# Gate and up by seven half-size products of sums of blocks, and down in a second pass

## The chip, the cores and the metric

The kernel runs on one core of one Trainium2 chip. The metric is the device time of an execution in microseconds (us). Engines are named as the profile names them: PE is TensorE's matmuls and PEld its weight loads, DVE is VectorE, ACT is ScalarE, POOL is GpSimd, SP is SyncE, which here only issues transfers.

## What is computed

One decoder layer in float32 for 512 tokens of width 2048: two kinds of attention side by side, their joint projection added to x, and then the feed-forward part, which is what the change touches:

```
x = x + mixed @ w_out[l]

h = rms_norm(x, ffn_norm_w[l])
x = x + (jax.nn.silu(h @ w_gate[l]) * (h @ w_up[l])) @ w_down[l]
return rms_norm(x, final_norm_w)
```

w_gate and w_up are 2048 x 5632, w_down is 5632 x 2048.

## The kernel before

Every product of float32 numbers is made as three matmuls in fp32r (mm3, line 143): each operand is split into a rounded part and a rest, and rounded x rounded, rounded x rest and rest x rounded are added in PSUM. For a weight the split is load_w (line 117): SP starts a transfer of 128 x 1024 floats (512 KB) into one of two buffers `raw`, ACT casts it to `whi` (line 137), DVE subtracts to get `wlo` (line 138); there are three pairs of whi and wlo, so a split can run ahead of PE by two loads.

x after attention (x2) lies in SBUF with tokens on partitions, 4 tiles of 128. out_part (line 714) adds the last pieces of the joint projection, 128 x 512 at a time; its last call is for four chunks of 512 columns. x2_split (line 857) transposes a chunk of x2 on PE, scales it by ffn_norm_w and splits it into `fh`, `fl`: features of the model on partitions, 512 tokens along the row. The division by the norm is left to later: `rbc` holds it for each token along a row, `rstd` for each token on a partition.

The feed-forward part goes by 11 groups of 512 hidden features. gate_up (line 884) takes a group in two pairs of 256 features, gate first and then up; I call gate or up of 256 features a unit, and there are 44. A unit loads four pieces of weights and makes 2 x 16 x 3 = 96 matmuls of 512 columns into two banks. Evicting a gate is a product with rbc on DVE and a Silu on ACT, evicting an up is a product with the gate and a split into `ah`, `al`. down (line 914) follows one group behind: for each chunk of 512 output columns two loads of w_down, 48 matmuls, and four additions to x2 on DVE. The last group of down is fused with the final norm.

What each engine does is a queue in the order that the program's scheduler made of the code; an instruction that waits holds up what stands behind it. ACT has casts, evictions and a few transfers in one queue, DVE splits and evictions, SP the transfers of weights. A tile's buffer is taken again when its last reader is over, in the order of the code.

Of the kernel before, what the change touches and what calls it, by code (L numbers as in the profile page):

```python
# [9 lines left out]
F32 = mybir.dt.float32  # L10
# [79 lines left out]
def layer_kernel(ctx: ExitStack, tc: tile.TileContext, x, positions, w_in, a_log, dt_bias, w_uq, w_ukv,  # L90
# [51 lines left out]

    def mm3(ps, lh, ll, rh, rl, start, stop):
        nc.tensor.matmul(ps, lhsT=lh, rhs=rh, start=start, stop=False)  # L144
        nc.tensor.matmul(ps, lhsT=lh, rhs=rl, start=False, stop=False)  # L145
        nc.tensor.matmul(ps, lhsT=ll, rhs=rh, start=False, stop=stop)  # L146

# [36 lines left out]
    def pool(stack, name, bufs=1, side=None):  # L184
        return stack.enter_context(tc.tile_pool(name=name, bufs=bufs, side=side, reuse_waits="tile"))
# [118 lines left out]

    ba = const.tile([P, NT, 16], F32, name="ba")

# [19 lines left out]

    sc = const.tile([P, 10, NT, NH], F32, name="sc")
    ea, tt_, ab, e_, z_, pl, beta, g_, gc, dec = (sc[:, i] for i in range(10))
    egc = const.tile([P, NT, NH], F32, name="egc")
    egl = const.tile([P, NT, NH], F32, name="egl")  # L330

# [363 lines left out]
    banks(op=1, score=3, acc=2, bank=2)  # L695
    x2 = pool(right, "x2", side="right").tile([P, NT, D], F32, name="x2")
# [4 lines left out]
    mgp = {"b": pool(mla_right, "mgb", side="right")}  # L701
    for c in range(4):
# [144 lines left out]
    mla_left.close()  # L847
    mix_stack.close()


    banks(acc=4, bank=4)
    fpool = pool(left, "ffn")
    fh = fpool.tile([P, KD, S], F32R, name="fh")
    fl = fpool.tile([P, KD, S], F32R, name="fl")
    jo = fpool.tile([P, S], F32, name="jo")
# [12 lines left out]
    mla_right.close()  # L868


    ap_ = pool(left, "act", bufs=2)
    fin = ap_.tile([P, D], F32, name="fin", bufs=1)
    nc.scalar.dma_start(fin, final_norm_w.rearrange("(o d) -> o d", o=1).broadcast_to([P, D]))

    def x2_rstd():
        nc.vector.tensor_reduce(out=st4[:, 0:4], in_=ssx, op=ALU.add, axis=AX.X)
        nc.vector.tensor_scalar(out=st4[:, 0:4], in0=st4[:, 0:4], scalar1=1.0 / D, scalar2=EPS,
                                op0=ALU.mult, op1=ALU.add)
        rsq(rstd, st4[:, 0:4])
        rows_of(ap_, rstd, rbc, "dg")  # L880

    NG = NFF // 4

    def gate_up(g):
        ah = ap_.tile([P, 4, S], F32R, name="ah", tag="ah")
        al = ap_.tile([P, 4, S], F32R, name="al", tag="al")
        for pr in range(2):
            c0 = g * S + pr * 256
            gs = []
            for w_v in (wg_v, wu_v):  # L890
                a2 = [acc() for _ in range(2)]
                for kk in range(4):
                    if g == 0 and pr == 0 and w_v is wg_v and kk == 3:
                        x2_split(3)
                        x2_rstd()
                    wh, wl = load_w(w_v[:, 4 * kk:4 * kk + 4, c0:c0 + 256], 4, 256)
                    for f in range(2):
                        fs = slice(f * P, (f + 1) * P)
                        for j in range(4):
                            k = 4 * kk + j  # L900
                            mm3(a2[f], wh[:, j, fs], wl[:, j, fs], fh[:, k, :], fl[:, k, :], k == 0, k == KD - 1)
                for f in range(2):
                    if w_v is wg_v:
                        s = ap_.tile([P, S], F32, name="sg", tag="sg", bufs=4)
                        nc.vector.tensor_tensor(out=s, in0=a2[f], in1=rbc, op=ALU.mult)
                        nc.scalar.activation(s, s, AF.Silu)
                        gs.append(s)
                    else:
                        s = gs[f]
                        nc.vector.tensor_tensor(out=s, in0=a2[f], in1=s, op=ALU.mult)  # L910
                        split(ah[:, 2 * pr + f, :], al[:, 2 * pr + f, :], s)
        return ah, al

# [12 lines left out]

    prev = None
# [74 lines left out]
```

## Time and profile before

| | before |
|---|---|
| runs | 2427.9, 2429.2, 2432.1 us, median 2429.2 |
| profiled execution | 2431.8 us, span of the records 2430.0 us |
| PE, PEld | 2377.5 us (98%), 1954.5 us (80%) |
| DVE, ACT, POOL | 1137.5 us (47%), 706.8 us (29%), 84.6 us (3%) |
| read from HBM | 219.5 MB, 92 GB/s over the span |

Busy time of an engine is the time in which one of its instructions ran; for PE the ends of matmuls are modelled, and they overlap, so the distance from one start to the next is the price of one in a stream, not its duration. In the feed-forward part, from 978 us on, gate and up take 44 units and down 11 groups; the last group with the final norm begins at 2375 us.

### The profile page before, as it was taken

The page shows a single profiled execution, that of the slowest core. Times are in us where ns is not written, and L with a number is a line of the kernel's source. Part 1 is how long each engine was busy: PE and PEld are TensorE (multiplying, and loading weights), DVE is VectorE, ACT ScalarE, POOL GpSimd, SP SyncE. Part 2 cuts the span into 40 slices and gives each one's busy share as a digit, 9 for nine tenths or more (in the row PEclk, how much of TensorE's full clock was granted, in tenths as well). Part 3 has the DMA queues.
Part 4 walks back from the last instruction along what each step waited for, and adds up shares of the span by engine and source line. Part 5 has one row for each costly group of instructions (what it writes and reads, how often), then busy time and mean ns, then how long its engine had stood idle before and what let it go on. Part 6 is the DMA issues. An engine that isn't in the chain of part 4 may idle for free.

```text
span 2430.0 us, 27609 instructions
## 1 busy us (share of the span) xinstructions
PE 2377.5 (98%) x11142; PEld 1954.5 (80%) x11142; DVE 1137.5 (47%) x1850; ACT 706.8 (29%) x1155; POOL 84.6 (3%) x89
## 2 busy tenths in 40 slices
PE   8999999999999999999999999999999999999998
PEld 6777878787787778888888888888888888888886
DVE  6556565655556555433434343433333343434345
ACT  5333333332333334322222212222222222222223
POOL 0010101110000000000000000000000000000000
PEclk9999999999999999999999999999999999999999
DMA  5322322222422222333333333232333333333333
GB/s 168 89 62 70 88 70 80 78 80 78 143 61 67 73 65 87 104 96 100 99 95 96 96 95 101 90 104 87 104 93 103 98 96 95 95 97 95 104 96 112
DMA packets 199807, 225.74 MB, mean 93 GB/s; under 512 B 17280, under 2 KB 161920, under 8 KB 199552
## 3 DMA queue, kind: packets, MB, share of 16 engines
q1 hardware_dynamic: 194752, 214.02, 29.4%
q10 hardware_dynamic: 4928, 9.97, 1.3%
q8 instruction: 87, 1.43, 0.3%
q14 instruction: 40, 0.33, 0.0%
HBM read 219.50 MB, written 4.46 MB: 92 GB/s over the span
## 4 chain that ended last, share of the span: by engine, by line
PE 87%; DVE 6%; DMA 3%; ACT 2%; issue 1%; POOL 1%; ACTq 0%; SPq 0%; POOLq 0%; DVEq 0%
PE acc L145 20%; PE acc L146 20%; PE acc L144 20%; PE bank L145 6%; PE bank L146 6%; PE bank L144 6%; PE bank L149 4%; DVE wlo L138 1%; PE score L149 1%; DMA rep<-dr 1%; DMA raw<-in_w_down 1%; PE op L149 1%; DVE y L444 1%; DMA raw<-in_w_in 1%; ACT whi L137 0%
## 5 line engine op out<-in xcount | busy, mean ns | idle before, releaser
L138 DVE TENSOR_TENSOR wlo<-raw,whi 128x1024 fp32r<-128x1024 f32 x386 | 469.0, 1216 | 705.7 <-ACT whi L137 701.0
L137 ACT CAST whi<-raw 128x1024 fp32r<-128x1024 f32 x386 | 403.6, 1046 | 1195.2 <-PE acc L145 650.0
L145 PE MATMUL acc<-fl,whi 128*128 128x512 f32 x1408 | 548.3, 389 | 0.0
L146 PE MATMUL acc<-fh,wlo 128*128 128x512 f32 x1408 | 548.2, 389 | 0.0
L144 PE MATMUL acc<-fh,whi 128*128 128x512 f32 x1408 | 548.1, 389 | 0.0
L145 PEld LDWEIGHTS acc<-fl,whi 128*128 128x128 f32 x1408 | 264.4, 188 | 54.8
L146 PEld LDWEIGHTS acc<-fh,wlo 128*128 128x128 f32 x1408 | 264.4, 188 | 54.8
L144 PEld LDWEIGHTS acc<-fh,whi 128*128 128x128 f32 x1408 | 264.3, 188 | 54.5
L145 PE MATMUL acc<-hl,whi 128*128 128x512 f32 (+1 forms) x656 | 264.4, 403 | 0.0
L144 PE MATMUL acc<-hh,whi 128*128 128x512 f32 (+1 forms) x656 | 262.1, 400 | 1.8 <-ACT whi L137 1.8
L146 PE MATMUL acc<-hh,wlo 128*128 128x512 f32 (+1 forms) x656 | 263.6, 402 | 0.0
L146 PE MATMUL bank<-whi,al 128*128 128x512 f32 x640 | 249.2, 389 | 0.0
L145 PE MATMUL bank<-wlo,ah 128*128 128x512 f32 x640 | 249.2, 389 | 0.0
L144 PE MATMUL bank<-whi,ah 128*128 128x512 f32 x640 | 249.2, 389 | 0.0
L924 DVE SCALAR_TENSOR_TENSOR x<-bank,rstd,x 128x512 f32<-128x512 f32 x160 | 119.8, 750 | 151.6 <-PE bank L146 151.6
L144 PEld LDWEIGHTS acc<-hh,whi 128*128 128x128 f32 (+1 forms) x656 | 124.3, 190 | 25.7 <-ACT whi L137 2.2
L145 PEld LDWEIGHTS acc<-hl,whi 128*128 128x128 f32 (+1 forms) x656 | 124.3, 190 | 24.5
L146 PEld LDWEIGHTS acc<-hh,wlo 128*128 128x128 f32 (+1 forms) x656 | 123.9, 189 | 23.5
L144 PEld LDWEIGHTS bank<-whi,ah 128*128 128x128 f32 x640 | 120.2, 188 | 24.9
L145 PEld LDWEIGHTS bank<-wlo,ah 128*128 128x128 f32 x640 | 120.2, 188 | 24.9
L146 PEld LDWEIGHTS bank<-whi,al 128*128 128x128 f32 x640 | 120.2, 188 | 24.9
L144 PE MATMUL acc<-whi,mgh 128*128 128x512 f32 x256 | 102.3, 400 | 2.8 <-ACT mgh L283 2.3
(284 smaller groups left out, 2228.1 us busy)
## 6 DMA issues: line engine op xcount, KB each, us to landing
raw<-in_w_gate SPq DMA_DIRECT2D x88, 512.0 KB, 3.6
raw<-in_w_up SPq DMA_DIRECT2D x88, 512.0 KB, 3.6
raw<-in_w_down SPq DMA_DIRECT2D x88, 512.0 KB, 3.8
raw<-in_w_in SPq DMA_DIRECT2D x80, 512.0 KB, 3.8
raw<-in_w_out SPq DMA_DIRECT2D x32, 512.0 KB, 4.0
rep<-dr ACTq DMA_DIRECT2D x8, 512.0 KB
x<-in_x ACTq DMA_DIRECT2D x4, 1024.0 KB, 7.8
raw<-in_w_ukv SPq DMA_DIRECT2D x32, 128.0 KB, 2.5
```

The source lines that it names most:

```text
L137: nc.scalar.copy(hi[:, :k * n], raw[:, :k * n])
L138: nc.vector.tensor_tensor(out=lo[:, :k * n], in0=raw[:, :k * n], in1=hi[:, :k * n].bitcast(F32), op=ALU.subtract)
L144: nc.tensor.matmul(ps, lhsT=lh, rhs=rh, start=start, stop=False)
L145: nc.tensor.matmul(ps, lhsT=lh, rhs=rl, start=False, stop=False)
L146: nc.tensor.matmul(ps, lhsT=ll, rhs=rh, start=False, stop=stop)
L149: nc.tensor.matmul(ps, lhsT=l, rhs=r, start=start, stop=stop)
L444: nc.vector.scalar_tensor_tensor(out=y, in0=u[:, j:j + S], scalar=vec[:, 0, j * 24 + ct:j * 24 + ct + 1], in1=y, op0=ALU.mult, op1=ALU.add)
L924: nc.vector.scalar_tensor_tensor(out=x2[:, t4, cs], in0=a, scalar=rstd[:, t4:t4 + 1], in1=x2[:, t4, cs], op0=ALU.mult, op1=ALU.add)
```

## The change

The product of a unit, 256 features by 2048 by 512 tokens, is written as a product of 2 x 2 blocks: the weights' two halves of features by even and odd blocks of the contraction, the activations' even and odd blocks by two halves of the tokens. Such a product is made with seven products of blocks in place of eight: four sums of weight blocks (s1 to s4), four sums of activation blocks (made once for all units), and seven sums of results, of which some are made by going on adding in a bank (`further` marks this in mm3). Each of the seven is 8 x 3 = 24 matmuls of 256 columns.

The seven activation operands, split, take 114 KB of each partition (`ch`, `cl`). So x2 is stored in DRAM (x2d), the products of gate and up are too (actd, a tile for each group), and down runs when all units are over: each group's activations are loaded and split (act_group), x2 is loaded again, and then down and the tail are as before. A unit's weights come in four transfers into one of two large buffers (wraw, 2 MB).

Left out of the diff: four small tiles (ba, sc, egc, egl) that move from one pool to another, the pool of mgb, which now outlives ckv, and mm3's new argument.

```
+    banks(acc=2, x=2, y=1, z=1, bank=2)
+    ch = cb.tile([P, N7, KD // 2, H], F32R, name="ch")
+    cl = cb.tile([P, N7, KD // 2, H], F32R, name="cl")
...
-    def x2_split(c):
-        for k in range(4 * c, 4 * c + 4):
+    def operands(i):
+        tps = []
+        for k in (2 * i, 2 * i + 1):
             tp = bank()
             for t4 in range(NT):
                 nc.tensor.transpose(tp[:, t4 * P:(t4 + 1) * P], x2[:, t4, k * P:(k + 1) * P], ident)
-            split(fh[:, k, :], fl[:, k, :], tp, fw[:, k:k + 1])
+            tps.append(tp)
+        st = tr.tile([P, N7, H], F32, name="stg", tag="stg", bufs=1)
+        wa, wb = fw[:, 2 * i:2 * i + 1], fw[:, 2 * i + 1:2 * i + 2]
+        nc.scalar.mul(st[:, 0, :], tps[0][:, 0:H], wa)
+        nc.scalar.mul(st[:, 5, :], tps[0][:, H:S], wa)
+        nc.scalar.mul(st[:, 1:3, :].rearrange("p a n -> p (a n)"), tps[1], wb)
+        for o, x, y in ((3, 5, 0), (5, 2, 5), (4, 2, 3), (6, 1, 4)):
+            nc.vector.tensor_tensor(out=st[:, o, :], in0=st[:, x, :], in1=st[:, y, :], op=ALU.subtract)
+        split(ch[:, :, i, :], cl[:, :, i, :], st)
 
     for c in range(4):
         out_part(12, mg_b, c, jo)
+        nc.scalar.dma_start(x2d[c].rearrange("p (t n) -> p t n", t=NT), x2[:, :, c * S:(c + 1) * S])
         if c:
-            x2_split(c - 1)
+            operands(2 * c - 2)
+            operands(2 * c - 1)
+    operands(6)
+    operands(7)
...
+    def unit(w_v, c0, dst):
+        raw = wr.tile([P, KD, 2 * P], F32, name="wraw", tag="wraw")
+        for kk in range(4):
+            nc.sync.dma_start(raw[:, 4 * kk:4 * kk + 4, :], w_v[:, 4 * kk:4 * kk + 4, c0:c0 + 2 * P])
...
+        def product(ps_, w, m, start=False):
+            hi = wp.tile([P, 1024], F32R, name="whi", tag="whi").rearrange("p (i n) -> p i n", n=P)
+            lo = wp.tile([P, 1024], F32R, name="wlo", tag="wlo").rearrange("p (i n) -> p i n", n=P)
+            split(hi, lo, w)
+            for i in range(KD // 2):
+                mm3(ps_, hi[:, i, :], lo[:, i, :], ch[:, m, i, :], cl[:, m, i, :],
+                    start and i == 0, i == KD // 2 - 1, not start)
...
+        product(X, a11, 0, True)
+        p1 = kept(X, "p1")
+        s1 = sum_of(a21, a22, ALU.add)
+        s2 = sum_of(s1, a11, ALU.subtract, "sw")
+        product(Z, a12, 1, True)
+        added(0, 0, Z, p1)
+        product(X, s2, 4)
+        u2 = kept(X, "u2")
+        product(Y, s1, 3, True)
+        p5 = kept(Y, "p5")
+        product(X, sum_of(a11, a21, ALU.subtract), 5)
+        added(1, 1, X, p5)
+        product(Y, sum_of(a12, s2, ALU.subtract), 2)
+        added(0, 1, Y, u2)
+        product(X, a22, 6)
+        nc.scalar.copy(dst[:, 1, 0:H], X)
...
+    for u in range(NFF // 2):
+        g, o = divmod(u, 2)
+        s = gu.tile([P, 2, S], F32, name="sg", tag="sg", bufs=2)
+        unit(wg_v, u * 2 * P, s)
...
+        nc.scalar.activation(s, s, AF.Silu)
+        t = gu.tile([P, 2, S], F32, name="up", tag="up")
+        unit(wu_v, u * 2 * P, t)
+        nc.vector.tensor_tensor(out=s, in0=t, in1=s, op=ALU.mult)
+        nc.scalar.dma_start(actd[g].rearrange("p (k n) -> p k n", n=S)[:, 2 * o:2 * o + 2, :], s)
...
+    def act_group(g):
+        ah = ad.tile([P, 4, S], F32R, name="ah", tag="ah")
+        al = ad.tile([P, 4, S], F32R, name="al", tag="al")
+        v = actd[g].rearrange("p (k n) -> p k n", n=S)
+        for o in (0, 2):
+            dst = tuple(t_[:, o:o + 2, :].rearrange("p k n -> p (k n)") for t_ in (ah, al))
+            load_w(v[:, o:o + 2, :], 2, S, dst)
+        return ah, al
+    cur = act_group(0)
...
+    for c in range(4):
+        nc.scalar.dma_start(x2[:, :, c * S:(c + 1) * S], x2d[c].rearrange("p (t n) -> p t n", t=NT))
...
-    for g in range(NG):
-        cur = gate_up(g)
-        if prev is not None:
-            down(g - 1, *prev)
-        prev = cur
+    for g in range(NG - 1):
+        nxt = act_group(g + 1)
+        down(g, *cur)
+        cur = nxt
```

Here kept copies a bank to SBUF on ACT, added adds such a copy and a bank on DVE into the unit's result, and sum_of adds or subtracts two weight blocks on DVE; ad holds two buffers each of ah and al.

Three places show what stands in the queues. On SP, from the last gate and up on, before:

```order
L135 DMA raw<-in_w_up 128x4x256 x4
L135 DMA raw<-in_w_down 128x2x512 x8
L135 DMA raw<-in_w_gate 128x4x256 x4
L135 DMA raw<-in_w_up 128x4x256 x4
L135 DMA raw<-in_w_gate 128x4x256 x4
L135 DMA raw<-in_w_up 128x4x256 x4
L135 DMA raw<-in_w_down 128x2x512 x16
```

and on SP for the last groups of down in the change (actd is the tile of one group's activations in DRAM):

```order
L135 DMA raw<-in_w_down 128x2x512 x8
L135 DMA raw<-actd_7538 128x1024 x2
L135 DMA raw<-in_w_down 128x2x512 x8
L135 DMA raw<-actd_7539 128x1024 x2
L135 DMA raw<-in_w_down 128x2x512 x8
L135 DMA raw<-actd_7540 128x1024 x2
L135 DMA raw<-in_w_down 128x2x512 x16
```

Down's weights no longer alternate with those of gate and up, but with the next group's activations, through the same two buffers. On ACT in the change, from the last weights of down(0) to the first of down(1); in brackets are the engines and transfer queues (DMAHW) that each waits for:

```order
L137 CAST whi<-raw 128x1024 [waits DMAHW4_49,DVE_49,PE_49]
L137 CAST whi<-raw 128x1024 [waits DMAHW5_49,DVE_49,PE_49]
L137 CAST ah<-raw 128x1024 [waits DMAHW6_49,PE_49]
L137 CAST ah<-raw 128x1024 [waits DMAHW7_49]
L137 CAST whi<-raw 128x1024 [waits DMAHW0_49,DVE_49]
L137 CAST whi<-raw 128x1024 [waits DMAHW1_49,DVE_49]
L137 CAST whi<-raw 128x1024 [waits DMAHW2_49,DVE_49,PE_49]
```

The two casts of the next group's activations (ah) stand ahead of down(1)'s first weights, and the first of them waits for PE. On ACT where gate and up begin, before (fh is the split of x2's last chunk):

```order
L286 ACTIVATE fh<-bank,vec 128x512 x4
L137 CAST whi<-raw 128x1024 x4
L286 ACTIVATE fh<-bank,vec 128x512 x4
L906 ACT_TABLE_LOAD
L906 ACTIVATE sg<-sg 128x512
```

and in the change (stg is the staging tile of operands, vec the norm's weights):

```order
L882 ACTIVATE stg<-bank,vec 128x256
L883 ACTIVATE stg<-bank,vec 128x256
L884 ACTIVATE stg<-bank,vec 128x512
L284 CAST ch<-stg 128x7x256
L882 ACTIVATE stg<-bank,vec 128x256
L883 ACTIVATE stg<-bank,vec 128x256
L884 ACTIVATE stg<-bank,vec 128x512
L284 CAST ch<-stg 128x7x256
L284 CAST whi<-wraw 128x1024 x2
L284 CAST whi<-sw 128x1024
```

Where casts of gate weights stood ahead of the last split of x2, all operands now stand ahead of the first weights.

## Rows read from the trace of the kernel before

**Rows 1.** The page: busy time by engine, granted clock in 40 slices, chain by engine.
```profile
PE 2377.5 (98%) x11142; PEld 1954.5 (80%) x11142; DVE 1137.5 (47%) x1850; ACT 706.8 (29%) x1155; POOL 84.6 (3%) x89
...
PEclk9999999999999999999999999999999999999999
...
PE 87%; DVE 6%; DMA 3%; ACT 2%; issue 1%; POOL 1%; ACTq 0%; SPq 0%; POOLq 0%; DVEq 0%
```

**Rows 2.** Timeline of gate and up: start, duration (us), engine, line, operation, out<-in.
```profile
978.60 0.39 PE L144 MATMUL acc<-fh,whi 128*128 128x512 f32 x1
...
984.94 0.39 PE L145 MATMUL acc<-fl,whi 128*128 128x512 f32 x1
...
1043.57 0.69 DVE L905 TENSOR_TENSOR sg<-acc,rbc 128x512 f32<-128x512 f32 x1 [0.64 <-PE acc L146]
...
1065.33 0.69 DVE L910 TENSOR_TENSOR sg<-acc,sg 128x512 f32<-128x512 f32 x1 [0.63 <-PE acc L146]
```

**Rows 3.** Timeline of PE in v_pair, 21 rows between.
```profile
667.02 0.28 PE L145 MATMUL acc<-wlo,ckh 128*128 128x256 f32 x1
...
669.66 0.28 PE L146 MATMUL acc<-whi,ckl 128*128 128x256 f32 x1
```

**Rows 4.** Instructions by line and shape: count | busy us, mean ns of one.
```profile
L138 DVE TENSOR_TENSOR wlo<-raw,whi 128x1024 fp32r<-128x1024 f32 x380 | 464.6, 1223 | 691.9 <-ACT whi L137 687.3 <-PE bank L861 4.2
...
L571 DVE TENSOR_TENSOR R<-R,bank 128x256 f32<-128x256 f32 x16 | 6.7, 421 | 23.6 <-PE bank L149 23.6
...
L137 ACT CAST whi<-raw 128x1024 fp32r<-128x1024 f32 x380 | 399.7, 1052 | 1160.7 <-PE acc L145 641.4 <-PE bank L146 248.9 <-issue 196.6
...
L556 ACT COPY T<-bank 64x256 f32<-64x256 f32 x8 | 2.9, 365 | 24.2 <-PE bank L555 24.2
```

**Rows 5.** Timeline: x2's load, and the passage from out_part to gate.
```profile
632.54 2.20 ACTq L703 DMA_DIRECT2D x<-in_x  x4
...
977.26 0.68 DVE L723 TENSOR_TENSOR x<-acc,x 128x512 f32<-128x512 f32 x1
...
978.67 2.40 ACT L286 ACTIVATE fh<-bank,vec 128x512 fp32r<-128x512 f32 x4
...
1003.45 0.69 DVE L905 TENSOR_TENSOR sg<-acc,rbc 128x512 f32<-128x512 f32 x1 [1.80 <-PE acc L146]
```

**Rows 6.** Timeline of the tail; transfers of L135, landing after issue.
```profile
2379.35 1.23 DVE L138 TENSOR_TENSOR fl<-raw,fh 128x1024 fp32r<-128x1024 f32 x1 [2.13 <-ACT fh L137]
...
2380.60 0.37 SPq L135 DMA_DIRECT2D raw<-in_w_down  x1
...
2382.98 0.50 PE L144 MATMUL bank<-fh,ah 128*128 128x512 f32 x1 [0.92 <-ACT fh L137]
...
2384.43 1.05 ACT L137 CAST fh<-raw 128x1024 fp32r<-128x1024 f32 x1 [0.88 <-DMA raw<-in_w_down]
...
DMA to landing us min/median/max: 3.3/3.7/11.0
```

**Rows 7.** Window: length, busy us by engine, granted clock, DMA share, GB/s.
```profile
8.00:12.00 4.00, 2.85 (x14) 2.85 (x15) 1.30 (x3) 1.53 (x3) 0.00 (x0) 1.00 1.08 377
```

**Rows 8.** Timeline of PE at the start and the end, and a window.
```profile
14.59 0.79 PE L144 MATMUL acc<-hh,whi 128*128 128x512 f32 x1 [1.77 <-ACT whi L137]
...
16.04 0.63 PE L145 MATMUL acc<-hl,whi 128*128 128x512 f32 x1
16.46 0.63 PE L146 MATMUL acc<-hh,wlo 128*128 128x512 f32 x1
...
21.13 0.39 PE L144 MATMUL acc<-hh,whi 128*128 128x512 f32 x1
21.36 0.39 PE L145 MATMUL acc<-hl,whi 128*128 128x512 f32 x1
...
2420.48 0.39 PE L146 MATMUL bank<-fh,al 128*128 128x512 f32 x1
...
2424.00:2428.00 4.00, 0.00 (x0) 0.00 (x0) 0.48 (x2) 0.93 (x2) 0.00 (x0) 0.50 0.78 253
```

More of the change, by code (lines that the diff above doesn't have):

```diff
@@ L141, in load_w, with mm3 @@
                 lo[:, :k * n].rearrange("p (k n) -> p k n", k=k))
[L143 to L146, printed above, removed]
+    def mm3(ps, lh, ll, rh, rl, start, stop, further=False):
+        nc.tensor.matmul(ps, lhsT=lh, rhs=rh, start=start, stop=False, skip_group_check=further)
+        nc.tensor.matmul(ps, lhsT=lh, rhs=rl, start=False, stop=False, skip_group_check=further)
+        nc.tensor.matmul(ps, lhsT=ll, rhs=rh, start=False, stop=stop, skip_group_check=further)
     def mm(ps, l, r, start=True, stop=True):
@@ L302, in row @@
         return gd.tile([P, S], F32, name="s_" + name, tag=name, bufs=bufs)
-    ba = const.tile([P, NT, 16], F32, name="ba")
+    ba = gd.tile([P, NT, 16], F32, name="ba", tag="ba", bufs=1)
     def narrow():
@@ L695, in layer_kernel @@
     banks(op=1, score=3, acc=2, bank=2)
-    x2 = pool(right, "x2", side="right").tile([P, NT, D], F32, name="x2")
+    x2_stack = right.enter_context(ExitStack())
+    x2 = pool(x2_stack, "x2", side="right").tile([P, NT, D], F32, name="x2")
+    mix_right = right.enter_context(ExitStack())
+    mgp = {"b": pool(mix_right, "mgb", side="right")}
     mla_right = right.enter_context(ExitStack())
@@ L700, in layer_kernel @@
     ckl = ckp.tile([P, NT, S], F32R, name="ckl")
-    mgp = {"b": pool(mla_right, "mgb", side="right")}
     for c in range(4):
@@ L848, in layer_kernel @@
     mix_stack.close()
[L851 to L855, printed above, removed]
-    def x2_split(c):
-        for k in range(4 * c, 4 * c + 4):
+    mla_right.close()
+    banks(acc=2, x=2, y=1, z=1, bank=2)
+    H = S // 2
+    N7 = 7
+    dram2 = ctx.enter_context(tc.tile_pool(name="dram2", bufs=1, space=bass.MemoryType.DRAM))
+    x2d = [dram2.tile([P, NT * S], F32, name=f"x2d{c}", tag=f"x2d{c}") for c in range(4)]
+    NG = NFF // 4
+    actd = [dram2.tile([P, 4 * S], F32, name=f"actd{g}", tag=f"actd{g}") for g in range(NG)]
+    cb_stack = left.enter_context(ExitStack())
+    cb = pool(cb_stack, "cb")
+    ch = cb.tile([P, N7, KD // 2, H], F32R, name="ch")
+    cl = cb.tile([P, N7, KD // 2, H], F32R, name="cl")
+    tr_stack = left.enter_context(ExitStack())
+    tr = pool(tr_stack, "tr")
+    jo = tr.tile([P, S], F32, name="jo", tag="jo", bufs=1)
+    def operands(i):
+        tps = []
+        for k in (2 * i, 2 * i + 1):
             tp = bank()
@@ new lines, in layer_kernel @@
+    operands(6)
+    operands(7)
+    nc.vector.tensor_reduce(out=st4[:, 0:4], in_=ssx, op=ALU.add, axis=AX.X)
+    nc.vector.tensor_scalar(out=st4[:, 0:4], in0=st4[:, 0:4], scalar1=1.0 / D, scalar2=EPS,
+                            op0=ALU.mult, op1=ALU.add)
+    rsq(rstd, st4[:, 0:4])
+    rows_of(tr, rstd, rbc, "jo")
+    mix_right.close()
+    x2_stack.close()
+    tr_stack.close()
+    gu_right = right.enter_context(ExitStack())
+    gu = pool(gu_right, "gu", side="right")
+    wr_right = right.enter_context(ExitStack())
@@ new lines, in layer_kernel, with half, sum_of, kept @@
+    wr = pool(wr_right, "wr", bufs=2, side="right")
+    def unit(w_v, c0, dst):
+        raw = wr.tile([P, KD, 2 * P], F32, name="wraw", tag="wraw")
+        for kk in range(4):
+            nc.sync.dma_start(raw[:, 4 * kk:4 * kk + 4, :], w_v[:, 4 * kk:4 * kk + 4, c0:c0 + 2 * P])
+        rv = raw.rearrange("p (i k) (f n) -> p i k f n", k=2, f=2)
+        a11, a12, a21, a22 = (rv[:, :, k, f, :] for f in range(2) for k in range(2))
+        def half(tag):
+            return pbank(tag)[:, 0:H]
+        def sum_of(x, y, op, tag="raw"):
+            t = (wp.tile([P, 1024], F32, name="raw", tag="raw", bufs=2) if tag == "raw"
+                 else gu.tile([P, 1024], F32, name="sw", tag="sw"))
+            t = t.rearrange("p (i n) -> p i n", n=P)
+            nc.vector.tensor_tensor(out=t, in0=x, in1=y, op=op)
+            return t
+        def product(ps_, w, m, start=False):
[5 more added lines that the diff above has]
+                    start and i == 0, i == KD // 2 - 1, not start)
+        def kept(ps_, name):
+            t = gu.tile([P, H], F32, name=name, tag=name, bufs=2)
+            nc.scalar.copy(t, ps_)
+            return t
+        def added(f, t, ps_, other):
+            nc.vector.tensor_tensor(out=dst[:, f, t * H:(t + 1) * H], in0=ps_, in1=other, op=ALU.add)
+        X, Z, Y = half("x"), half("z"), half("y")
+        product(X, a11, 0, True)
[14 more added lines that the diff above has]
+        nc.scalar.copy(dst[:, 1, 0:H], X)
@@ new lines, in layer_kernel @@
+    wr_right.close()
+    banks(bank=8)
+    ad_right = right.enter_context(ExitStack())
+    ad = pool(ad_right, "ad", bufs=2, side="right")
+    def act_group(g):
[6 more added lines that the diff above has]
+        return ah, al
@@ L871, in layer_kernel @@
+    cur = act_group(0)
+    cb_stack.close()
     ap_ = pool(left, "act", bufs=2)
+    x2 = ap_.tile([P, NT, D], F32, name="x2b", tag="x2b", bufs=1)
     fin = ap_.tile([P, D], F32, name="fin", bufs=1)
+    fh = ap_.tile([P, KD, S], F32R, name="fh", tag="fh", bufs=1)
+    fl = ap_.tile([P, KD, S], F32R, name="fl", tag="fl", bufs=1)
+    for c in range(4):
+        nc.scalar.dma_start(x2[:, :, c * S:(c + 1) * S], x2d[c].rearrange("p (t n) -> p t n", t=NT))
     nc.scalar.dma_start(fin, final_norm_w.rearrange("(o d) -> o d", o=1).broadcast_to([P, D]))
[L875 to L912, printed above, removed]
```

11 lines of the change are left out of this document (6 added, 5 removed).

## Prediction

> **What bounds the kernel now.** I read the page first: PE is busy for 98% of the span, the granted clock is full in every slice, and the chain that ended last is PE for 87% [rows 1]. So a stage is worth what its matmuls cost, and an idle PE is lost time one for one. Then the stage that changes: from one eviction of a gate to that of the up behind it is 21.76 us [rows 2], and the unit between them (256 features of gate or of up, 512 tokens) is 96 matmuls of 512 columns, 0.2267 us each; 28 steps of the trace give 0.2264 [rows 2]. Nothing else is waited for there. Then the price of a matmul of 256 columns: 22 steps in v_pair take 2.64 us, 0.120 each [rows 3], 6% above half of a full one.
>
> **The units.** There are 44. The order of the change shows seven products of 24 matmuls, 168 of 256 columns: 168 x 0.120 = 20.16 us, 1.60 less than 21.76; 44 x 1.60 = 70.4 us gained, if PE stays the bound. DVE gets seven splits and four sums of 1024 columns, 1.22 each, one more pass of that size (times rbc, or gate times up), and three sums of 256 at 0.42: 16.0 us [rows 4]. ACT gets seven casts at 1.05, four copies at 0.37 and in a gate unit a Silu taken at 1.06: 9.9 us. Both fit. In time, too: three pairs of whi and wlo let a split begin when the product three back is over, two products (5.76 us) early, for 2.3 us of cast and split. The narrowest place is p1, the copy of the first product: on ACT it stands behind the cast of the fourth weight and the Silu, 2.88 + 1.05 + 1.06 + 0.37 = 5.36 us into the unit, and the third product needs it at 5.76. I take no stall; up to 10 us over all units stays in the range.
>
> The Trainium skill (TensorE: Matmul & The Clock Gate, Back-to-back issue gap) gives N/2.4 GHz plus 2.5 ns for a step, 215.8 and 109.2 ns here, and by it the gain would be 44 x 2.37 = 104 us; the rows show 226.7 and 120 for these very forms, and the rows decide.
>
> **Into gate and up: 39 us lost.** Before, gate weights were there when out_part ended, and the last x2_split ran inside the first gate unit: from the last x2 eviction to the second gate eviction is 26.2 us, 4.4 above a plain unit [rows 5]. Now operands(i) runs eight times through one staging tile: three copies from PSUM (0.37, 0.37, 0.60), three subtractions that wait for the third (1.26), a cast of 1792 columns (1.74 by the slope of the ACT rows), a split of the same (2.02 by DVE's), and only then the next: 6.4 us [rows 4, 5]. During out_part's last two chunks DVE has 12.6 us a chunk (adds, splits and two operands) against 12.8 of PE with its transposes, so I charge nothing there (bound 5 us), and the four stores of x2 take ACT about 0.55 each to issue [rows 5], inside that. When out_part's last matmul ends, I have operands(3) half done, 7 us of it left (the rstd chain stands in DVE's queue there), and four to go: 7 + 25.6 = 32.6. The first gate weights, on SP, wait for the last split of all, since their buffer lies over memory of the staging pool. They are 2.1 MB in four transfers: a lone 512 KB transfer takes 3.83 us to its cast [rows 6], of which 1.4 at the 377 GB/s seen with several under way [rows 7], so 2.4 + 5.6 = 8.0. Then a sum and a split stand before PE's third matmul, 2.4. That is 43; four early matmuls (0.5), the old 4.4 and 1.4 of transposes now made in the gap come off, and 2.3 of slow clock (below) comes on: 39. Bounds: 33 (faster hand-overs, no slow clock) to 50 (four transfers one by one, 14 us).
>
> **Into down: 12 us.** down(0) needs two act groups split and then w_down, all through two raw buffers. Walking back from the last product's end E: the second group's halves land at about E - 0.3 and E + 0.9, but ACT has the last copy, the stores and five reload transfers to issue (about 0.5 each), so the second is cast at E + 5.8. w_down's first half starts at E + 2 beside x2's reload and is cast at E + 6.8; its second half starts at E + 8 beside 5 MB and is split at E + 15. PE then has 29 of 48 matmuls left, so the first chunk ends at E + 21.6 in place of 10.9: 10.7, plus 1.3 of clock. Bounds 8 and 17, by the share of the rate that w_down gets.
>
> **Between down groups: 9 x 10.2 = 92 us.** This is the term that decides. act_group(g + 1) is written ahead of down(g), so its two transfers take both raw buffers, and its casts wait for the ah that down(g - 1) reads to its end. On ACT the casts of down(g)'s weights stand behind these two, on SP their transfers behind the buffers. Let the last matmul of a group start at S. The reader before it ends at S + 0.2; casts to S + 1.25 and S + 2.3; splits on DVE to S + 2.5 and S + 3.65. Only then do the first two w_down transfers start. The tail of the trace has this very chain: a split ends at 2380.58, the transfer starts at 2380.60, its cast at 2384.43 [rows 6]. So the first cast runs from S + 6.3, PE starts at S + 7.4 (it is released by a cast, as at 2382.98 [rows 6]), does two matmuls and waits for the split until S + 8.6, where it should have been at S + 0.7: 7.9 us. The second half is ready at S + 9.8 and costs nothing more. It happens ahead of down(1) to down(9): 9 x 7.9 = 71. Bounds by the transfer, 3.3 (the shortest [rows 6]) to 4.2: 7.4 to 8.3 each.
>
> After each such pause comes **the clock**. PE's last matmul starts at 2420.48, and in 2424 to 2428 the granted clock is 0.50: 1.2 GHz [rows 8]. At the start of the trace matmuls step by 0.42 us at 16.5 and by 0.23 at 21.1 [rows 8], so what resumed at 14.6 ran at half rate for up to 6 us, a loss of up to 3. No pause of 7 us occurs mid-kernel in this trace, so the price of one lies between 0 and 3; I take 2.3, near the start's: 9 x 2.3 = 21.
>
> A rule speaks against this change here: the Trainium skill (TensorE: Matmul & The Clock Gate, Why this matters for your kernels) says that idle gaps between bursts of matmuls send the clock back to half. Without it the sum is 25 us lower.
>
> Tail, down's own chunks and everything ahead of out_part's last chunks keep their order; I charge nothing. The kept tiles that moved from one pool to another change no queue.
>
> **Sum.** 2431.8 (profiled run) - 70.4 + 39 + 12 + 71 + 21 = 2504; that run lay 2.6 above the median: **2502 us**.
>
> **Rivals.**
> - *The clock does not fall in the pauses* (its fall is only in the records of the end): 2502 - 25 = 2477.
> - *The pauses between down groups are not there*, and the kernel gets faster. Mechanism: w_down's first pieces are in SBUF when the group before ends, so that only the casts of ah (2.3 us, beside PE) are late; price 92 us, time 2410. It decides from a pause of 2.1 us on, since -70.4 + 39 + 12 leaves 19 us for nine. For it: w_down's transfers are short and DMA is mostly idle. Against it: two raw buffers, both held by the act group until the end of the group before, as the order shows.
> - *DVE becomes the bound of a unit.* Its inputs there are runs of 128 in rows of 512, which no row of the trace has. From 26% dearer on (16.0 to 20.16) it decides; at 40% a unit is 21.4 and the time 2556.
> - *A half-size matmul costs half*, 0.113: 168 x 0.113 = 19.0, 50 us more gained, 2452. This is nearest to what the page's formula says (0.506 of a full step). The 22 steps of [rows 3] speak against it.
> - That the products are not seven is out: the order counts them.
>
> **Chances.** Forecast 0.72; clock stays up 0.12; DVE bound 0.06; half price 0.02; no pauses 0.05; the rest is a larger start of gate or down. The range 2465 to 2538 takes the forecast from its low ends (33 and 8 at the two starts, pauses of 7.4, no slow clock) to its high ones (50, 17, 9 x 11.2, 10 of stalls), and the first rival; DVE, half price and no pauses are left out. Within 0.2% (about 5 us, what a measurement of this kernel can tell) would take a coincidence: 0.02. Faster: 0.05, slower 0.93.
>
> **What would show it.** A gate or up unit of 20.2 us with PE's steps at 0.12 and no idle time inside; one idle stretch of some 40 us ahead of the first product, ended by the weights' transfer; nine stretches of 7 us between down groups in which ACT casts ah, then SP's transfer runs; a granted clock of 0.5 just behind them. The forecast is wrong if the down groups follow each other without such stretches, or if units take over 20.5 us.

## The result, and the profile after

| | before | after |
|---|---|---|
| runs, us | 2427.9 to 2432.1, median 2430.2 | 2506.0 to 2509.9, median 2508.5 |
| ratio | | 1.032 (95% interval 1.030 to 1.034) |
| span of the profiled execution | 2430.0 us | 2507.7 us |

The change makes the kernel 3.2% slower. The forecast was 2502. Times and ratios, here and below, leave out two disturbed executions, one of run 12's kernel (4591 us) and one of the kernel before (8302 us). First the page of after: busy time by engine and granted clock in 40 slices [rows 1].

```profile
PE 2345.4 (94%) x14310; PEld 2067.5 (82%) x14310; DVE 1565.9 (62%) x2248; ACT 899.6 (36%) x1435; POOL 83.4 (3%) x89
...
PEclk9999999999999997899999999999998999899999
```

PE is busy for 32 us less than before and the span is 78 us longer, so some 110 us of idle PE are new. The clock row dips at the start of gate and up, at the entry into down and once more within down.

The units, one line of after (the copy that ends each unit of a gate, one unit in two): duration in ns, first and last start in us.

```profile
L962 ACT COPY sg<-x x22: 366/366/366, 1039.5 to 1886.4; 128x256 f32<-128x256 f32 x22
```

From 1039.5 to 1886.4 are 42 units: 20.16 us each, in place of 21.76 [rows 2]. Nothing in between waits. That is 44 x 1.60 = 70 us gained.

The chain of after from out_part's end to the first product: start, duration, what.

```profile
972.16 0.24 PE acc L147
...
977.15 1.94 DVE cl L285
...
983.65 2.04 DVE cl L285
...
1003.43 2.04 DVE cl L285
...
1005.84 0.37 SPq L916
...
1014.91 2.00 ACT whi L284 x2
```

Four more operands follow the one at 977.15 (the next at 983.65, the last at 1003.43), 6.6 us each, and only behind the last does the transfer of the gate weights start (SPq, 1005.84), 9.1 us to its cast. The first unit ends with the copy at 1039.5; before, it ended with the eviction at 1003.45 [rows 5]. 36.1 later, in a unit that is 1.6 shorter: 37.6 us lost.

The entry into down: ACT of after, then the first matmuls of down on PE. ACTq rows are transfers that ACT issues; fin holds the final norm's weights, and an act half is one of the two loads of a group's activations.

```profile
1905.76 0.59 ACTq L999 DMA_DIRECT2D x2b<-x2d  x1
1906.34 0.36 ACT L962 COPY up<-x 128x256 f32<-128x256 f32 x1
...
1909.23 3.30 ACTq L999 DMA_DIRECT2D x2b<-x2d  x3
1912.57 2.27 ACTq L1000 DMA_DIRECT2D fin<-in_final_norm_w  x1
1914.87 1.04 ACT L137 CAST ah<-raw 128x1024 fp32r<-128x1024 f32 x1 [8.16 <-issue]
1915.83 1.04 ACT L137 CAST whi<-raw 128x1024 fp32r<-128x1024 f32 x1
1926.47 1.04 ACT L137 CAST whi<-raw 128x1024 fp32r<-128x1024 f32 x1 [9.60 <-DMA raw<-in_w_down]
```

```profile
1916.92 1.65 PE L145 MATMUL bank<-whi,ah 128*128 128x512 f32 x3 [11.20 <-ACT whi L137]
```

PE idles for 11.2 us until 1916.92, so the last product ended at 1905.7, and group 0's weights are cast 10.1 and 20.8 us behind it. Its last matmul starts at 1970.01 (below), 64.3 us behind, where 191 steps of 0.2267 us make 43.3: the entry costs 21.0 us. (The expectations below have 20.5, counted from just ahead of the copy that starts at 1906.34.) No eviction waits for x2 here; all that DVE's evictions wait for in down is PE:

```profile
L1012 DVE SCALAR_TENSOR_TENSOR x2b<-bank,rstd,x2b 128x512 f32<-128x512 f32 x160 | 119.9, 750 | 189.8 <-PE bank L147 189.8
```

The boundary between groups 0 and 1 of down, all engines of after; then one line of a whole tile, and windows (length, busy PE, granted clock, DMA share, GB/s).

```profile
1970.01 0.39 PE L147 MATMUL bank<-whi,al 128*128 128x512 f32 x1
1970.21 1.99 ACT L137 CAST ah<-raw 128x1024 fp32r<-128x1024 f32 x2 [10.96 <-PE bank L146]
...
1971.28 2.36 DVE L138 TENSOR_TENSOR al<-raw,ah 128x1024 fp32r<-128x1024 f32 x2
1972.54 13.26 SPq L135 DMA_DIRECT2D raw<-in_w_down  x5
1976.40 1.04 ACT L137 CAST whi<-raw 128x1024 fp32r<-128x1024 f32 x1 [4.20 <-DMA raw<-in_w_down]
...
1977.50 1.22 PE L145 MATMUL bank<-whi,ah 128*128 128x512 f32 x2 [7.10 <-ACT whi L137]
...
1979.78 0.63 PE L145 MATMUL bank<-whi,ah 128*128 128x512 f32 x1
1980.20 0.63 PE L146 MATMUL bank<-wlo,ah 128*128 128x512 f32 x1
```

```profile
L147 PE MATMUL bank<-whi,al x640: 387/389/632, 1919.0 to 2453.1; 128*128 128x512 f32 x160
```

```profile
1970.00:1972.00 2.00, 0.40 (x2) 1.00 0.00 0
...
1976.00:1978.00 2.00, 0.50 (x1) 0.50 0.62 236
...
1980.00:1982.00 2.00, 2.00 (x6) 0.50 0.85 258
1982.00:1984.00 2.00, 2.00 (x8) 0.76 0.63 231
```

The casts of ah wait for the group before, the splits behind them hand the raw buffers back, only then SP's transfer starts, and PE stands for 7.1 us. Behind it matmuls step by 0.42 us, at a granted clock of 0.50 (1.2 GHz), and by 0.23 before 1984. From the last matmul of group 0 to that of group 9 are 2453.1 - 1970.0 = 483.1 us, for 9 x 43.5 = 391.7 of matmuls: 91.4 us over nine boundaries, 10.2 each.

Sum: -70.2 + 37.6 + 21.0 + 91.4 = 79.8; the spans differ by 77.7. The 2.1 between are the tail: from the last matmul of group 9 to the end of the span are 54.6 us in after, and 56.8 before (2373.2 to 2430.0).

### The profile page after: what moved, and what is told of

Its sections match the earlier page's. It is cut to its first block, busy times and chain, and to the rows that moved or that the text cites. A ratio compares the mean times of both kernels' runs of the same rounds, so it can differ in the third digit from the quotient of the medians.

```text
span 2507.7 us, 35015 instructions
## 1 busy us (share of the span) xinstructions
PE 2345.4 (94%) x14310; PEld 2067.5 (82%) x14310; DVE 1565.9 (62%) x2248; ACT 899.6 (36%) x1435; POOL 83.4 (3%) x89
## 4 chain that ended last, share of the span: by engine, by line
PE 81%; DVE 7%; DMA 5%; ACT 3%; issue 2%; POOL 1%; ACTq 0%; SPq 0%; POOLq 0%; DVEq 0%
PE x L147 7%; PE x L145 7%; PE x L146 7%; PE acc L146 7%; PE acc L147 7%; PE acc L145 7%; PE bank L145 6%; PE bank L146 6%; PE bank L147 6%; PE bank L150 4%; PE y L147 3%; PE y L146 3%; PE y L145 3%; DMA raw<-in_w_down 2%; PE z L145 2%
## 5 line engine op out<-in xcount | busy, mean ns | idle before, releaser
L137 ACT CAST whi<-raw 128x1024 fp32r<-128x1024 f32 (+1 forms) x210 | 218.2, 1039 | 578.4 <-PE bank L147 233.5
L145 PE MATMUL x<-ch,whi 128*128 128x256 f32 x1408 | 399.4, 284 | 14.1 <-ACT whi L284 14.1
L146 PE MATMUL x<-cl,whi 128*128 128x256 f32 x1408 | 399.1, 283 | 0.0
L147 PE MATMUL x<-ch,wlo 128*128 128x256 f32 x1408 | 399.1, 283 | 0.0
L138 DVE TENSOR_TENSOR wlo<-raw,whi 128x1024 fp32r<-128x1024 f32 (+1 forms) x210 | 253.4, 1208 | 194.4 <-ACT whi L137 193.8
L145 PEld LDWEIGHTS x<-ch,whi 128*128 128x128 f32 x1408 | 271.1, 193 | 14.5 <-ACT whi L284 14.4
L146 PEld LDWEIGHTS x<-cl,whi 128*128 128x128 f32 x1408 | 271.1, 193 | 0.0
L147 PEld LDWEIGHTS x<-ch,wlo 128*128 128x128 f32 x1408 | 271.0, 192 | 0.0
L284 ACT CAST whi<-raw 128x1024 fp32r<-128x1024 f32 x132 | 138.5, 1050 | 200.2 <-PE x L146 152.4
L146 PE MATMUL y<-cl,whi 128*128 128x256 f32 x704 | 199.2, 283 | 0.0
```

What stands on the lines that cost most here:

```text
L137: nc.scalar.copy(hi[:, :k * n], raw[:, :k * n])
L138: nc.vector.tensor_tensor(out=lo[:, :k * n], in0=raw[:, :k * n], in1=hi[:, :k * n].bitcast(F32), op=ALU.subtract)
L284: nc.scalar.copy(dst_h, src)
```

## The experiments

The kernel before was run beside each; ratios are to it. A median of 2508.5 below is the change itself.

**1. Act groups later, all but the first.**

```
     for g in range(NG - 1):
-        nxt = act_group(g + 1)
-        down(g, *cur)
+        nxt = None if g else act_group(g + 1)
+        nxt = down(g, *cur, nxt)
...
         for c in range(4):
+            if c == 2 and nxt is None:
+                nxt = act_group(g + 1)
```

> The act group of the next group is written between the second and third chunk of the running down group, in place of ahead of its first, for all groups but the first one (so the entry into down stays). Theory (the pause is the two raw buffers held by the act group until the group before has ended): the nine stretches between groups, 91 us together in the trace of the change, go, clock loss with them, and 2508 becomes 2417; up to 1.5 us may come back in each group because the act halves now take two turns of the raw buffers between weights, so 2417 to 2430. Rival (what the group boundary waits for is the trip through DRAM or the casts of ah behind their reader): the stretches only move to the third chunk, and the time stays above 2490. A second rival, that the slow clock has another cause than the idle time, would leave some 20 of the 91 us: 2437.

Measured: 2421.9 us, ratio 0.997 (0.996 to 0.998). All nine boundaries are gone: in its trace the last evictions of groups 0 and 8 (1974.38, 2322.74) are 348.4 us apart, eight times 43.5. PE's wait for the casts of weights in down, total, times, longest, first after and then this run:

```profile
PE bank L145 <- ACT whi L137: 80.4, 11, 11.2
```

```profile
PE bank L145 <- ACT whi L137: 14.9, 2, 10.9
```

What is left is the entry. So the boundary was the order of loads through two buffers, neither the trip through DRAM nor the casts of ah, and the kernel turns from 3.2% slower to 0.3% faster with it.

**2. PE kept busy in the pause.**

```
+    dm = ap_.tile([P, 384], F32R, name="dm", bufs=1)
+    nc.scalar.copy(dm, rbc[:, 0:384])
     def down(g, ah, al):
+        if g:
+            idle = bank()
+            for _ in range(38):
+                mm(idle[:, 0:384], dm[:, 0:P], dm)
```

> The changed kernel with 38 matmuls of 384 columns added on PE ahead of groups 1 to 9 of down, on data that is in SBUF, into a bank that nobody reads: they stand in the pause of some 7.1 us and take some 6.5. Theory (PE's rest is what brings the granted clock to 0.50, and the first 12 or so matmuls behind the pause pay for it): the clock stays at 1.00 through the boundaries, and of the 10.1 us per boundary 2 to 3 go: 2508 less 18 to 27 is 2481 to 2490. Rival (the half clock comes from something else, such as the burst of transfers at the boundary, or these matmuls push the real ones back): 2508 or more.

Measured: 2491.9 us, ratio 1.025 (1.023 to 1.027), 16.6 below the change. The same boundary in its trace:

```profile
1973.54 6.78 PE L150 MATMUL bank<-dm 128*128 128x384 f32 x38
...
1980.77 1.19 PE L145 MATMUL bank<-whi,ah 128*128 128x512 f32 x4 [0.45 <-ACT whi L137]
...
1982.59 0.40 PE L145 MATMUL bank<-whi,ah 128*128 128x512 f32 x1
1982.83 0.39 PE L146 MATMUL bank<-wlo,ah 128*128 128x512 f32 x1
```

```profile
1980.00:1982.00 2.00, 1.50 (x6) 1.00 0.32 124
```

The weights come at the same distance, but the clock is 1.00 and the steps 0.23. The last evictions of groups 0 and 9 (1973.74, 2436.97) are 463.2 us apart, 71.5 over nine boundaries in place of 91.4: 2.2 us of each boundary were the clock. The Trainium skill (TensorE: Matmul & The Clock Gate, Why this matters for your kernels) says that idle gaps between bursts send the clock back; these two traces agree (0.50 behind a rest of 7.1 us, 1.00 where 0.45 us of it was left). The time fell by less than these 20 us, and by 1.4 less than the least that was expected; the entry of this trace is 2.7 longer.

**3. Four more additions on DVE in each unit.**

```
+        def extra():
+            w = raw.rearrange("p k n -> p (k n)")
+            t = gu.tile([P, 384], F32, name="ex", tag="ex")
+            for i in range(2):
+                nc.vector.tensor_tensor(out=t, in0=w[:, 0:384], in1=w[:, 1024:1408], op=ALU.add)
...
+        extra()
         product(X, s2, 4)
...
+        extra()
         product(X, a22, 6)
```

> The changed kernel with four more additions of 384 columns on DVE in every unit of gate and up, some 0.55 us each, 2.2 in all, whose result nobody reads: DVE then has 18.2 of the unit's 20.16 us. Theory (PE is the bound of a unit, and splits are made two products ahead): within 10 us of 2508. Rival (DVE's queue is already as late as PE can bear, so that what is added there comes out at PE): up to 44 x 2.2 = 97 us more, 2550 to 2605.

Measured: 2515.0 us, ratio 1.035 (1.033 to 1.037): 6.5 more, where DVE got 75 more (busy 1641.0 us for 1565.9, 1.7 a unit and not 2.2). PE's waits in the units of its trace, total, times, longest (in after there are none):

```profile
PE x L145 <- ACT p L946: 6.6, 6, 1.8
```

PE is the bound of a unit: with DVE at some 17.1 of 20.16 us (677.3 in the 800 us from 1100 on) it waits six times in all. The place that gives first is the copy of the first product.

**4. Two staging tiles, splits behind the next operand's copies.**

```
-    operands(6)
-    operands(7)
+    mix_right.close()
+    tr2 = pool(st_stack, "tr2", bufs=2, side="right")
+    late = [operands(4, tr2)]
+    for i in (5, 6, 7):
+        late.append(operands(i, tr2))
+        late.pop(0)()
+    late.pop()()
```

(operands returns its split to be called later; 4 and 5 are no longer in the loop.)

> The last four operands get two staging tiles of their own over the memory of the last mixer group, and each one's cast and split is written behind the copies and subtractions of the next. Theory (the single staging tile makes each operand a chain of 6.6 us, five of which lie on the path after the last matmul of the output projection): a step falls to what DVE has, 1.3 of subtractions and 2.0 of split with hand-overs, some 3.5 to 4.2 us, so that 4 x 2.5 = 10 us go (8 to 12): 2496 to 2500. Rival (the copies, PE's transposes through two banks, or the weights' transfer set the start): under 3 us.

Measured: 2498.5 us, ratio 1.028 (1.026 to 1.030), 10 less, as expected. In its trace the last split is over at 993.8 in place of 1005.5, and the weights then take until 1004.9:

```profile
989.88 3.94 DVE cl L285 x2
...
995.72 8.99 DMA wraw<-in_w_gate
...
1004.87 2.00 ACT whi L284 x2
```

**5. Weight buffers over x2's memory.**

```
-    gu_right = right.enter_context(ExitStack())
-    gu = pool(gu_right, "gu", side="right")
     wr_right = right.enter_context(ExitStack())
     wr = pool(wr_right, "wr", bufs=2, side="right")
+    gu_right = right.enter_context(ExitStack())
+    gu = pool(gu_right, "gu", side="right")
```

> The weight buffers of gate and up are placed over the memory of x2 (free when the last operand's transposes have read it) in place of memory that holds the staging tile. Theory (the 9.4 us from the last split to the first cast of gate weights are a transfer that stands behind the chain of operands only because of the memory): the first transfers start some 8 us earlier and run beside the last operand, 2508 becomes 2499 to 2502. Rival (PE then waits for something else at the start, such as the order on ACT): over 2504.

Measured: 2499.6 us, ratio 1.029 (1.027 to 1.030), 9 less, as expected. The transfer now starts at 994.8, behind the last transposes, and the first cast comes at 1004.2 in place of 1014.9:

```profile
994.77 0.37 SPq L916
...
1004.17 2.00 ACT whi L284 x2
```

**6. Act groups later, all.** As 1, with `None` for the first group too.

> As the run before, but for the first group too, so that at the entry into down the weights of group 0 are loaded before the second act group. Theory: the entry, 20.5 us in the trace of the change (PE idle 11 us, then two matmuls' worth of work, then idle 5), comes from w_down's first two transfers standing behind two more act transfers and beside the reload of x2; with the act group out of the way the first weights are in SBUF when the last product ends and the entry falls to 3 to 10 us: 10 to 17 below the run before, 2400 to 2420. Rival (the reload of x2 alone fills the entry, since the first eviction needs it): within 3 us of the run before.

Measured: 2410.7 us, ratio 0.992 (0.991 to 0.993), 11 less than 1. PE goes on 1.0 us behind the last product, but stops twice within group 0. The first of these stops, and the window (columns as above) behind it:

```profile
1915.54 1.22 PE L145 MATMUL bank<-whi,ah 128*128 128x512 f32 x2 [2.73 <-ACT whi L137]
...
1916.00:1918.00 2.00, 1.96 (x5) 0.50 1.04 402
```

From the copy that ends the last unit to the start of group 0's last eviction are 55.1 us, where 43.3 would be without a wait: 11.8 late (20.8 late in after, 21.6 in run 1; I use this count below). So the order of the act group is worth some 10 us of the entry.

**7. The reload of x2 on SP, behind each chunk's weights, act groups as in the change.**

```
-    for c in range(4):
-        nc.scalar.dma_start(x2[:, :, c * S:(c + 1) * S], x2d[c].rearrange("p (t n) -> p t n", t=NT))
...
             ws = [load_w(wd_v[:, 4 * g + 2 * kk:4 * g + 2 * kk + 2, cs], 2, S) for kk in range(2)]
+            if g == 0:
+                nc.sync.dma_start(x2[:, :, cs], x2d[c].rearrange("p (t n) -> p t n", t=NT))
```

(The load of fin stands after group 0 in the code.)

> The changed kernel with its act groups where they are, but each chunk's reload of x2 is issued by SP behind that chunk's weights in group 0, and the final norm's weights come after the first group, so that ACT issues no transfers and w_down's first megabyte doesn't share the rate with 5 MB. Theory (of the entry's 20.5 us, some 10 are ACT's 6 us of issuing ahead of the second act half's cast, and the slow transfer of the first weights): the entry falls to 9 to 12, 2508 becomes 2497 to 2500. Rival (the entry is set by the act group alone, by its two turns of the raw buffers): 2505 or more.

Measured: 2505.8 us, ratio 1.031 (1.030 to 1.033). A miss by 6 us, and within the rival's range. The last product of its trace ends at 1908.7, and then, on ACT, on SP and in the chain of waits:

```profile
1908.72 0.34 ACTq L1019 DMA_DIRECT2D fin<-in_final_norm_w  x1
...
1912.11 1.04 ACT L137 CAST ah<-raw 128x1024 fp32r<-128x1024 f32 x1 [2.52 <-DVE sg L973]
```

```profile
1908.70 0.62 SPq L1004 DMA_DIRECT2D x2b<-x2d  x1
1910.60 0.40 SPq L135 DMA_DIRECT2D raw<-in_w_down  x1
1911.04 0.54 SPq L1004 DMA_DIRECT2D x2b<-x2d  x1
```

```profile
1910.60 10.05 DMA raw<-in_w_down
```

The second act half is cast 3.4 us behind the last product and no longer 9.2, so ACT's issuing is out of the way. But the scheduler put the first chunk's reload and fin ahead of the weights all the same, and the weights' 512 KB take 10 us beside 3 MB. Group 0 ends 15.2 us late in place of 20.8 (the median falls by 2.7 only; this execution came to down 2.9 later). The Trainium skill (Trainium Kernel Development and Optimization, Key Constraints) says that transfers issued from SP, ACT and POOL run on the same DMA engines and interleave, so that another queue saves only issue time; this pair of traces agrees (a load of w_down's 512 KB took 9.2 us in after with the reload on ACT's queue, and 10.05 here with it on SP's).

**8. The reload made to come late.** As 7, and in group 0:

```
+                seen = ws[1][1][0:1, 1, S - 1:S].bitcast(F32)
+                nc.vector.tensor_copy(x2[0:1, 0, c * S:c * S + 1], seen)
                 nc.sync.dma_start(x2[:, :, cs], x2d[c].rearrange("p (t n) -> p t n", t=NT))
+                if c == 3:
+                    nc.vector.tensor_copy(fin[0:1, 0:1], seen)
+                    nc.scalar.dma_start(fin, final_norm_w.rearrange("(o d) -> o d", o=1).broadcast_to([P, D]))
```

> As the run with late reloads, but the reloads now really come late: one element of each x2 chunk is first copied from the split of that chunk's second weight half, so that the reload cannot start before it (in the run before, two reloads and the final norm's weights were still issued within 2.4 us around the first transfer of w_down, which then took 10 us to its cast). Theory (at the entry w_down's transfer shares the rate with the reload, and this, more than ACT's issuing, is what I sized too small): the first half of w_down lands in some 4 us, the entry of 20.5 us falls to 11 to 13, 2508 becomes 2498 to 2502. Rival (the entry is set by the act group's two turns of the raw buffers, whatever else is under way): 2504 or more.

Measured: 2506.8 us, ratio 1.032 (1.030 to 1.034). A miss again, and again within the rival's range. In its trace (last product over at 1907.7) the weights come sooner, and DVE waits instead:

```profile
1913.91 1.04 ACT L137 CAST whi<-raw 128x1024 fp32r<-128x1024 f32 x1 [3.46 <-DMA raw<-in_w_down]
1917.61 1.04 ACT L137 CAST whi<-raw 128x1024 fp32r<-128x1024 f32 x1 [2.66 <-DMA raw<-in_w_down]
```

```profile
1927.22 2.07 DVE L1016 SCALAR_TENSOR_TENSOR x2b<-bank,rstd,x2b 128x512 f32<-128x512 f32 x3 [4.75 <-DMA x2b<-x2d]
...
1940.73 2.07 DVE L1016 SCALAR_TENSOR_TENSOR x2b<-bank,rstd,x2b 128x512 f32<-128x512 f32 x3 [6.93 <-DMA x2b<-x2d]
```

So the theory held for the weights (6.2 and 9.9 us behind the last product, where after has 10.1 and 20.8), and it fell for the time: the eviction needs x2, DVE's queue holds the next splits behind it, and group 0 ends 15.7 us late. Part of the price moved from the weights to the reload. The rival's part stays in both runs: the act group is still ahead of the weights, and the first of them is cast 6.2 us behind the last product even where no reload runs beside it.

**9 to 11. Everything together, three orders of group 0.** 4, 5 and 7's reload, one act half ahead of the second and one ahead of the fourth chunk of each group:

```
     def down(g, ah, al):
+        nxt, halves = act_group(g + 1, (1, 3))
         for c in range(4):
+            if c in halves:
+                halves.pop(c)()
```

> Everything together: two staging tiles with the splits behind the next operand's copies, weight buffers over x2, one act half written ahead of the second and one ahead of the fourth chunk of each down group, each chunk's reload of x2 on SP's queue behind its weights in place of all four on ACT's, and the final norm's weights after the first group. From 2410.7 (the run with all act groups late): less 10 (the run with two staging tiles measured that), less 8 (weight buffers), less 5 to 9 (entry to down: ACT's 5 us of issuing no longer stands ahead of the weights' casts), so 2383 to 2391, by 1.6 to 1.9 per cent below the kernel before. Rival (the gains overlap, since at the start the weights' transfer now overlaps the shorter chain, and the entry is set by the reload of x2): 2395 to 2402.

Measured: 2393.4 us, ratio 0.985 (0.984 to 0.987), above the range that I gave. The start gains 13.6 us (first casts at 1001.3), and not 18: the weights' transfer now starts at 991 behind the transposes, which come no earlier than 989, so 4 and 5 overlap as the rival had it, though the time lies under the rival's range too. Group 0 ends 10.3 late. Then with the act halves of group 0 ahead of the third and fourth chunk:

```
-        nxt, halves = act_group(g + 1, (1, 3))
+        nxt, halves = act_group(g + 1, (1, 3) if g else (2, 3))
```

> The run with everything together, but in group 0 the act halves are written ahead of the third and fourth chunk in place of the second and fourth, so that the weights of chunk 1 come ahead of them. In that run PE stood still for 5.4 us behind chunk 0 and went on at half clock, because the act half and the reload of x2 came before chunk 1's weights. Theory (these 5.4 us and the 2 of clock go): 2393 becomes 2385 to 2389. Rival (the reload of x2 alone fills that time, whatever stands in the raw buffers): 2391 to 2394.

Measured: 2392.9 us, ratio 0.985 (0.983 to 0.986): no gain. The stop behind chunk 0 stays, now with chunk 1's weights taking 12.2 us to land. And with the reload forced late as in 8:

> Everything together, with the act halves of group 0 ahead of the third and fourth chunk, and the reloads made to come late as in the run beside this. Theory: the hole of some 4 us behind chunk 0, in which chunk 1's weights took 12 us to land beside 2 MB of x2 and 1 MB of the final norm's weights, and the slow clock behind it (some 3 us) go: 2393 becomes 2384 to 2388. Rival (something else holds the second chunk): 2391 to 2394.

Measured: 2395.1 us, ratio 0.986 (0.984 to 0.987): no gain either; both forecasts fell, the first to its rival, the second past it by 1 us. DVE stands for the first chunk of x2, whose transfer takes 9 us in its chain of waits:

```profile
1896.37 9.01 DMA x2b<-x2d
```

**12. x2 not needed in group 0.** As the second of these, but group 0 evicts without x2, and x2 is added in groups 1 to 4:

```
+                if g == 0:
+                    nc.vector.tensor_scalar(out=x2[:, t4, cs], in0=a, scalar1=rstd[:, t4:t4 + 1],
+                                            scalar2=None, op0=ALU.mult)
...
+            if c == 0 and 0 < g < 6:
+                nc.vector.tensor_copy(fin[0:1, 0:1], ws[1][1][0:1, 1, S - 1:S].bitcast(F32))
+                nc.sync.dma_start(fin, x2d[g - 1] if g < 5 else
+                                  final_norm_w.rearrange("(o d) -> o d", o=1).broadcast_to([P, D]))
...
+        if 0 < g < 5:
+            for t4 in range(NT):
+                xs = x2[:, t4, (g - 1) * S:g * S]
+                nc.gpsimd.tensor_tensor(out=xs, in0=fin[:, t4 * S:(t4 + 1) * S], in1=xs, op=ALU.add)
```

> Everything together (the run with act halves of group 0 ahead of the third and fourth chunk), but group 0 of down writes its evictions without x2, and x2 comes back one megabyte at a time in groups 1 to 4, through the tile of the final norm's weights, and is added by GpSimd. In the four orders tried, group 0 ended 9.6 to 11.8 us late whenever the act group was out of its way, and in the traces either a transfer of weights lay beside the reload or DVE, with splits behind it in its queue, waited for the reload. Theory (what is left of the entry is the 4 MB reload being needed within group 0): group 0 ends 1 to 4 us late, and 2393 becomes 2384 to 2388. Rival (what is left is the switch from products to chunks itself, two raw buffers and casts in the same queues): 2390 to 2395.

Measured: 2385.9 us, ratio 0.982 (0.980 to 0.983), 7 below the run it is built on, within the forecast and faster than both kernels. Group 0 ends 1.9 us late, where the run it is built on has 9.6, and windows around the entry show a busy PE at full clock (columns as above):

```profile
1890.00:1894.00 4.00, 3.93 (x18) 1.00 0.46 147
1894.00:1898.00 4.00, 4.00 (x20) 1.00 0.75 248
```

The loads of x2 and of the final norm's weights within group 0 were what was left of the entry. The edit takes away both their share of the rate and the evictions' need of x2, so it doesn't part the two.

## Why the prediction was right, and where it was off

- **Units: right.** 20.16 us forecast and measured, 70 us gained. The price of a 256-column matmul from v_pair [rows 3] held in the units, so the rival at half price fell. Run 3 put aside DVE as the bound, and in after its sums, with inputs in runs of 128, take 1.22 us, as [rows 4] gave for such a size. (That rival's two figures don't fit together: 16.0 us made 40% dearer is 22.4, not 21.4.) The narrow place was named rightly, too.
- **Into gate and up: 39 forecast, 37.6 measured.** The chain took 6.6 us an operand for 6.4, the weights 9.1 for 8.0; that the sum came out lower all the same is luck: the last matmul of out_part starts at 972.0 in after and at 975.9 before, 3.9 us earlier, where I had taken off 1.4 for transposes. Runs 4 and 5 confirm both parts, one by one.
- **Between down groups: 92 forecast, 91.4 measured.** With S the start of the last matmul, the forecast had the transfer at S + 2.5, the first cast at S + 6.3, PE at S + 7.4; the trace has 2.5, 6.4 and 7.5. Run 1 shows that the cause is the order of loads, run 2 that 2.2 us of each (2.3 forecast) are the clock. The rival without a slow clock fell with run 2; the one without pauses came true only where the order was changed.
- **Into down: 12 forecast with bounds 8 and 17, 21.0 measured: the term that was mis-sized, beyond its upper bound.** The mechanism was right, act halves and then w_down through two raw buffers beside the reload, and the first transfer of w_down starts 2.0 us behind the last product, as forecast. Two steps of the walk failed. I charged ACT about 0.5 us for each of five transfers that it issues; they took 6.2 us in all, and the second act half was cast 9.2 us behind the last product, not 5.8. And I had the second half of w_down split 7 us behind its start; its transfer alone took 9.2. PE therefore stopped a second time, at 1922, and the clock fell a second time. The upper bound came from the share of the rate that w_down gets in one transfer, without ACT's issuing and without the second fall. Of group 0's lateness, the order of the act group makes some 10 us (run 6 against run 1: 21.6 to 11.8), and the loads of x2 and fin within group 0 some 8, once that order is out of the way (run 12 against run 10: 9.6 to 1.9). In after the reload acts as the forecast had it, as a neighbour of w_down; DVE's evictions wait for it only in runs 8 and 11, where it was forced late. How the 21 us of after divide between the two is not shown: with the reload moved in runs 7 and 8 and the act groups in their place, group 0 still ended 15.2 and 15.7 us late.
- **Sum.** The entry is 9.0 over, the start of gate and the boundaries 1.4 and 0.6 under, and the tail, charged at nothing, 2.2 under: 77.7 more where I had 72.6, and 2508 where I had 2502.

## What to carry to other kernels

A load that is written ahead of its time takes the buffers that the next thing on the path needs: with a rotating pair, an early load whose consumer must wait for old readers blocks all loads behind it. Here this cost more than the arithmetic saved, and moving one call from the head of a loop body to its middle was worth 87 us. A trip through DRAM is priced at the places where the data is needed again: its load shares the rate with the loads on the path, and an eviction that adds to an old value may wait for it (run 8). It can be kept off the path: let the first pass write without the old value and add it when the engines have room (run 12).

## What I had not expected of the hardware

- Issuing a transfer took ACT 2.27 us behind four reloads of 1 MB that it had issued in the 7 us before, and 0.34 us for the same transfer in run 7, where it had issued no reload; three reloads took 3.30 us to issue.
- A transfer of 512 KB, 3.8 us to its cast in the tail of before [rows 6], took 9.2 (after) to 12.2 us (run 10) beside 2 to 5 MB of others; one of 1 MB took 9.0 (run 11).
- In the entry of run 6 PE rested for 2.7 us (1912.8 to 1915.5) and went on at a granted clock of 0.50, as it did behind 7.1 us at a boundary of after; behind the 0.45 us that were left in run 2 the clock was 1.00.
